# Where the weights of the quarter products begin in SBUF, and a shift of all SBUF operands by 32 bytes

## The chip, the core and the metric

The kernel runs on one core of one Trainium2 chip. The metric is the device time of one launch in microseconds. Inputs are already in the chip's memory (HBM), and the output goes back there. A core has TensorE (PE in the profile; its weight loads are listed apart as PEld), VectorE (DVE), ScalarE (ACT), GpSimd (POOL) and SyncE (SP), which here only issues DMAs. All of them work on SBUF, an on-chip memory of 128 partitions; an address below is a byte's place within a partition. Matmul results go to PSUM.

## The reference

A decoder trunk of two layers on 512 tokens of width 1024. Layer 0 mixes tokens with a gated delta rule, layer 1 with sliding-window attention; each layer then has a SwiGLU feed-forward block with an inner width of 2816. Cut to what matters here:

```
D_MODEL = 1024
SEQ = 512
D_FF = 2816
...
def swiglu(h, w_gate_up, w_down):
    gu = h @ w_gate_up
    return (jax.nn.silu(gu[..., :D_FF]) * gu[..., D_FF:]) @ w_down
...
    for layer in range(DEPTH):
        h = rms_norm(x, ln_mix[layer])
        ...
        x = x + jnp.concatenate([mix_out.astype(x.dtype), mem_o.astype(x.dtype)], axis=-1) @ w_out[layer]
        x = x + swiglu(rms_norm(x, ln_ffn[layer]), w_gate_up[layer], w_down[layer])
```

## The kernel before

Activations lie with features on partitions and tokens along the row: a tile of 128 features by 512 tokens. There are eight such tiles for the width of 1024. A product of such tiles runs on TensorE as a series of matmuls, each with a block of weights of 128 x 128 (the stationary operand, loaded into the array first) and a moving operand of up to 512 tokens.

To keep float32 accuracy, every large operand is split in two parts in a shorter float32 format (`fp32r`): a high part that ScalarE copies, and a low part that VectorE gets by subtraction (`split`, L168). `mm3` (L198) then multiplies with three matmuls: high weights with high activations, high weights with low, low weights with high. In the profile `g<-h,whi` is a matmul into PSUM tile g with moving operand h and weights whi; `l` and `wlo` are the low parts.

Three kinds of such matmuls fill the kernel:

- Full-width products, 512 tokens to a matmul: the projections of both layers, the output projection (`row`, `output`), part of the gate and up products and the whole down product (`ffn`, L1190 to L1198). The weights lie in tiles `whi` and `wlo` from `part` (L195), at the tile's beginning.
- Quarter products, 256 tokens to a matmul (`quarters`, L1275). Most of the gate and up products are made from seven products of half-size blocks in place of eight, with sums of weights and sums of activations. The moving operands are halves of h and of tiles T (the sums of activations, `token_sums`, L1246). One call makes two feature tiles with 7 x 4 x 3 = 84 matmuls; the two layers have 38 calls.
- Half-width products at the start (memory tokens) and at the very end (L1213 to L1222, the last two feature tiles of the down product, one half of the tokens at a time).

The weights of a quarter product are 512 elements wide, and two of them share a tile of 1152 elements (D + P). `ring` (L1130) hands out six such places. A place is a view of T + P = 640 elements, and the weights take 512 of them, beginning at element `shift[0]`:

```
places.extend(tuple(x[:, i * T:(i + 1) * T + P] for x in two) for i in range(2))
places.append(places.pop(0))
return [x[:, shift[0]:shift[0] + T] for x in places[-1]]
```

`begin` (L1139) sets `shift[0]` to P - 8 = 120 elements, 480 bytes, before the first weights are placed, so all of them begin there.

Tiles come from pools that are stacked from the left end of SBUF (constants, weights, activations, x) and from the right end (`side="right"`: what one stage alone needs, such as T). `build` (L246) opens the pools. The order of instructions on each engine is the order of the code, with a few orders added by hand (`nosync`, L116); a recording layer adds the waits that the tiles' overlaps require. SP's queue issues nearly all loads in order.

Every engine's order is settled when the program is built, and so is every address. In the built program before the change, moving operands of all full-width and quarter products begin at byte 320 modulo 512; weights of full-width products at 320; weights of quarter products at 288.

Of the kernel before, what the change touches and what calls it, by code (L numbers as in the profile page):

```python
# [9 lines left out]
F32 = mybir.dt.float32  # L10
# [8 lines left out]
P = 128  # L19
# [67 lines left out]
class Builder:  # L87
# [158 lines left out]
    def build(self):  # L246
        tc, nc, a = self.tc, self.nc, self.a
        with ExitStack() as st:
            opened = lambda name, **kw: tc.tile_pool(name=name, bufs=1, reuse_waits="tile", **kw)
            pool = lambda name, **kw: st.enter_context(opened(name, **kw))  # L250
            cp = pool("const")
            self.wpool, self.apool = pool("w"), pool("acta")
            self.dpool = pool("scratch", space=DRAM)
            self.load_constants(cp)
            self.weng = nc.vector
            with opened("layer0", side="right") as self.mpool:
                with self.banks(pj=3, g=2, sc=3):
                    with opened("early", side="right") as ep:
                        self.mem_and_norm(ep)
                    with opened("gdn", side="right") as gp:  # L260
                        mix = self.gdn(gp)
                    self.bpool, xp = pool("actb"), pool("x")
                    self.x = [self.t(xp, [P, T], F32, f"x{k}") for k in range(KD)]
                    for k in range(KD):
                        nc.sync.dma_start(self.x[k], a["xT"][:, k, :])
                    self.rstd, self.cosT, self.sinT = (self.t(xp, [P, T], F32, n) for n in ("rstd", "cosT", "sinT"))
                    h = self.output(xp, 0, mix)
            with opened("ffn0", side="right") as fp, self.banks(pj=2, g=6):
                self.ffn(fp, xp, 0, h, self.apool, rope=True)
            with self.banks(pj=2, qk=2, pt=2), opened("swa", side="right") as sp:  # L270
                h = self.output(xp, 1, *self.swa(sp))
            with opened("ffn1", side="right") as fp, self.banks(pj=2, g=6):
                self.ffn(fp, xp, 1, h, self.bpool)
# [825 lines left out]
    def ffn(self, fp, xp, layer, h, apool, rope=False):  # L1099
# [4 lines left out]
        acts, sums, open_pairs, places, waiting, shift, sized = [], [], [], [], [], [0], []  # L1104
# [34 lines left out]
        def begin(f, up, by, tag, bufs, then):  # L1139

            o = [self.t(fp, [P, T], F32, tag, bufs) for _ in range(2)]
            steps = self.quarters(fp, [col(f + i, up) for i in range(2)], sums, by, o, ring)
            shift[0] = P - 8
            next(steps)
            while waiting:
                x = waiting.pop()
                self.nosync(self.fn(x, x, AF.Silu), self.held)
            end()
            next(steps)
            open_pairs.append((steps, then, o))  # L1150
            return o

        def end():
            if open_pairs:
                steps, then, o = open_pairs.pop()
                next(steps, None)
                for x in o:
                    then(x)
# [8 lines left out]
        for f0 in (0, half):  # L1167
# [7 lines left out]
            for f in range(f0 + 1, f0 + half, 2):  # L1175
                if f == 1:
                    g = []
                    for i in range(2):
                        for _ in range(2 - i):
                            sums.append(self.token_sums(fp, layer, len(sums), h))  # L1180
                        g.append(gate(f + i))
                    sums.append(self.token_sums(fp, layer, len(sums), h))
                else:
                    g = begin(f, 0, (self.rstd, self.rstd), "fg", 4, lambda x: self.fn(x, x, AF.Silu))
                begin(f, 1, g, "fu", 3, put)
# [432 lines left out]
```

## Time and profile before

| | |
|---|---|
| Time, median of 3 runs | 1130.85 us (1130.81 to 1131.25) |
| Span of the profiled execution, first to last instruction | 1129.4 us |
| TensorE busy | 1119.9 us, 99%, 7339 matmuls |
| VectorE busy | 827.6 us, 73% |
| ScalarE busy | 634.4 us, 56% |
| DMA traffic | 151.15 MB, mean 134 GB/s |

The profile is of one execution, which has a span of its own; what lies around the span (the difference to the times of the runs) isn't in the trace. Durations of matmuls in the rows (279 ns with 256 columns, some 390 with 512) include the time in which a result runs through the array, and they overlap: the rate is read from the starts of neighbouring matmuls, or from a piece of the chain, which gives a length and a number of matmuls. In rows of groups, `x636 | 251.7, 398 | 0.0` means 636 instructions, 251.7 us busy together, 398 ns each, and no idle time of the engine ahead of them.

### The profile page before, as it was taken

To read this page: it belongs to the slowest core of one execution; us is meant where nothing else is said; L and a number is where in the kernel's file an instruction comes from. 1 tells how busy PE (TensorE), PEld (TensorE's weight loads), DVE (VectorE), ACT (ScalarE), POOL (GpSimd) and SP (SyncE) were. 2 spreads that over 40 slices of the span, in tenths; PEclk is the share of its full clock that TensorE was granted. 3 is DMA by queue.
4 is the path that set the end of the run, shared out by engine and by line. 5 is a ranking of instruction groups with operands and counts; after the bars stand their busy time and mean duration, and the time that the engine had idled before them with its cause. 6 is when DMAs were issued, how large, how long until landed. Compare 5 with 4: busy or idle time off the path is not lost.

```text
span 1129.4 us, 19330 instructions
## 1 busy us (share of the span) xinstructions
PE 1119.9 (99%) x7339; PEld 986.1 (87%) x7339; DVE 827.6 (73%) x1553; ACT 634.4 (56%) x1285; POOL 73.2 (6%) x91
## 2 busy tenths in 40 slices
PE   9999999999999999999999999999999999999997
PEld 8888778887899988899988887788999988999986
DVE  7676976577888975588955877839999634889643
ACT  8588664456566632366643555856666422666434
POOL 0000000000021001011000000000111000111001
PEclk9999999999999999999999999999999999999999
DMA  8344252234567536377533321116687533776232
GB/s 314 109 153 149 95 131 86 85 113 145 174 167 195 143 111 169 102 191 195 134 89 102 132 75 38 53 43 180 158 201 185 144 103 105 173 190 156 77 103 87
DMA packets 72401, 151.15 MB, mean 134 GB/s; under 512 B 16956, under 2 KB 18516, under 8 KB 72308
## 3 DMA queue, kind: packets, MB, share of 16 engines
q1 hardware_dynamic: 60884, 129.21, 36.3%
q0 software_dynamic: 11136, 20.45, 11.2%
q8 instruction: 57, 0.93, 0.3%
q14 instruction: 36, 0.29, 0.1%
q10 hardware_dynamic: 288, 0.26, 0.1%
HBM read 142.94 MB, written 6.96 MB: 133 GB/s over the span
## 4 chain that ended last, share of the span: by engine, by line
PE 96%; DVE 2%; ACT 1%; DMA 0%; issue 0%; DVEq 0%; SPq 0%; ACTq 0%
PE pj L146 46%; PE g L146 38%; PE sc L146 6%; PE qk L146 3%; PE pt L146 2%; PE pt L150 1%; PE g L150 1%; DVE big L153 1%; DVE qv L156 0%; DVE btmp L153 0%; DMA early<-in_early 0%; DVE wlo L153 0%; ACT sm L134 0%; DVE T L153 0%; DVE gcr L153 0%
## 5 line engine op out<-in xcount | busy, mean ns | idle before, releaser
L140 ACT ACTIVATE whi<-wraw 128x512 fp32r<-128x512 f32 (+3 forms) x318 | 235.3, 748 | 240.6 <-PE pj L146 164.0
L153 DVE TENSOR_TENSOR wlo<-wraw,whi 128x512 fp32r<-128x512 f32 (+3 forms) x318 | 262.8, 837 | 92.7 <-ACT whi L140 85.2
L146 PE MATMUL pj<-h,whi 128*128 128x512 f32 (+1 forms) x652 | 256.4, 395 | 0.0
L146 PE MATMUL pj<-l,whi 128*128 128x512 f32 (+1 forms) x652 | 254.4, 390 | 0.0
L146 PE MATMUL pj<-h,wlo 128*128 128x512 f32 (+1 forms) x652 | 254.0, 390 | 0.0
L146 PE MATMUL g<-T,whi 128*128 128x256 f32 x1216 | 216.8, 279 | 0.0
L146 PEld LDWEIGHTS g<-T,whi 128*128 128x128 f32 x1216 | 185.1, 188 | 1.3 <-DVE fu L156 1.3
L146 PE MATMUL g<-T,wlo 128*128 128x256 f32 x608 | 169.7, 279 | 0.0
L146 PEld LDWEIGHTS pj<-h,whi 128*128 128x128 f32 x652 | 122.4, 188 | 28.0 <-issue 4.1
L146 PEld LDWEIGHTS pj<-h,wlo 128*128 128x128 f32 x652 | 122.5, 188 | 25.4 <-issue 0.9
L146 PE MATMUL g<-l,whi 128*128 128x256 f32 (+1 forms) x500 | 144.5, 289 | 0.0
L146 PE MATMUL g<-h,whi 128*128 128x256 f32 (+1 forms) x500 | 144.4, 289 | 0.0
L146 PE MATMUL g<-h,wlo 128*128 128x256 f32 (+1 forms) x500 | 144.4, 289 | 0.0
L146 PEld LDWEIGHTS pj<-l,whi 128*128 128x128 f32 x652 | 122.6, 188 | 23.6 <-DVE l L1468 0.3
L146 PEld LDWEIGHTS g<-T,wlo 128*128 128x128 f32 x608 | 114.3, 188 | 0.0
L146 PEld LDWEIGHTS g<-h,whi 128*128 128x128 f32 x500 | 94.0, 188 | 1.9
L146 PEld LDWEIGHTS g<-l,whi 128*128 128x128 f32 x500 | 93.9, 188 | 1.9
L146 PEld LDWEIGHTS g<-h,wlo 128*128 128x128 f32 x500 | 93.9, 188 | 1.8
L1286 POOL DMA_DIRECT2D ws<-in_wgu x38 | 33.5, 881 | 733.0 <-DMA ws<-in_wgu 399.1
L140 ACT ACTIVATE whi<-ws 128x512 fp32r<-128x512 f32 x76 | 48.0, 631 | 42.0 <-PE g L146 35.6
L153 DVE TENSOR_TENSOR wlo<-ws,whi 128x512 fp32r<-128x512 f32 x76 | 52.0, 684 | 5.9 <-ACT whi L140 5.9
L1287 POOL DMA_DIRECT2D ws<-in_wgu x38 | 34.2, 900 | 196.4 <-DVE wlo L153 71.4
(421 smaller groups left out, 1683.2 us busy)
## 6 DMA issues: line engine op xcount, KB each, us to landing
wraw<-in_wgu SPq DMA_DIRECT2D x50, 512.0 KB, 4.4
ws<-in_wgu SPq DMA_DIRECT2D x76, 256.0 KB, 3.4
ws<-in_wgu POOLq DMA_DIRECT2D x76, 256.0 KB, 4.5
wraw<-in_win SPq DMA_DIRECT2D x26, 512.0 KB, 3.6
wraw<-in_wdn SPq DMA_DIRECT2D x32, 384.0 KB, 3.1
wraw<-in_wdn SPq DMA_DIRECT2D x32, 320.0 KB, 2.9
wraw<-in_wgu SPq DMA_DIRECT2D x38, 256.0 KB, 4.0
wraw<-in_wout SPq DMA_DIRECT2D x16, 512.0 KB, 3.6
```

Source lines behind the costliest of these rows:

```text
L140: self.copied = self.nc.scalar.activation(out, in_, AF.Copy, **kw).ins
L146: return self.nc.tensor.matmul(out, lhsT, rhs, start=start, stop=stop, skip_group_check=more).ins
L150: return self.nc.tensor.transpose(out, in_, self.ident[:k, :k]).ins
L153: return eng.tensor_tensor(out=out, in0=a, in1=b, op=op).ins
L1286: nc.gpsimd.dma_start(s1, a22, accum_op=ALU.add)
L1287: nc.gpsimd.dma_start(s3, a21, accum_op=ALU.add)
```

## The change

Two unused tiles are added. One of 8 elements (32 bytes) follows the opening of the pool of constants at the left end, so that all tiles behind it on that side begin 32 bytes further up. One of 120 elements (480 bytes) lies at the right end, so that all tiles on that side begin 480 bytes further down. Both are +32 modulo 512. `shift[0]` goes from 120 elements to 16: the quarter products' weights begin 64 bytes into their places, not 480.

```
@@ -248,7 +248,9 @@
             opened = lambda name, **kw: tc.tile_pool(name=name, bufs=1, reuse_waits="tile", **kw)
             pool = lambda name, **kw: st.enter_context(opened(name, **kw))
+            self.t(pool("edge", side="right"), [P, 120], F32, "edge")
             cp = pool("const")
+            self.t(cp, [P, 8], F32, "edge")
             self.wpool, self.apool = pool("w"), pool("acta")
...
@@ -1140,7 +1142,7 @@
             steps = self.quarters(fp, [col(f + i, up) for i in range(2)], sums, by, o, ring)
-            shift[0] = P - 8
+            shift[0] = 16
             next(steps)
```

In the built program the starts become, modulo 512:

| matmuls | number | moving operand | weights |
|---|---|---|---|
| full width, 512 columns | 2526 | 320, then 352 | 320, then 352 |
| quarter products, 256 columns | 3192 | 320, then 352 | 288, then 416 |
| half width at the end and start | 132 | 320, then 352 | 320, then 352 |
| half width at the start | 96 | 192, then 224 | 320, then 352 |
| half width at the start | 72 | 320, then 352 | 192, then 224 |
| half width at the start | 24 | 96, then 128 | 192, then 224 |

The instructions and their order stay the same on all engines. One wait is added, since the tiles from the left and those from the right now meet at another place. On SP's queue ahead of layer 0's output projection, the loads of x (the residual stream) and of the output weights stood so:

```order
105 L265 DMA x_524_2732<-in_xT 128x512 [waits DMAHW7_49]
106 L265 DMA x_525_2733<-in_xT 128x512 [waits DMAHW0_49]
107 L265 DMA x_526_2734<-in_xT 128x512 [waits DMAHW1_49]
108 L179 DMA wraw_2944<-in_wout 128x1024 [waits DMAHW2_49,DVE_49]
109 L179 DMA wraw_2984<-in_wout 128x1024 [waits DMAHW3_49,DVE_49]
```

In the same place on SP's queue they now stand so:

```order
105 L267 DMA x_526_2737<-in_xT 128x512 [waits DMAHW7_49]
106 L267 DMA x_527_2738<-in_xT 128x512 [waits DMAHW0_49]
107 L267 DMA x_528_2739<-in_xT 128x512 [waits DMAHW1_49,PE_49]
108 L179 DMA wraw_2949<-in_wout 128x1024 [waits DMAHW2_49,DVE_49]
109 L179 DMA wraw_2989<-in_wout 128x1024 [waits DMAHW3_49,DVE_49]
```

The last load of x (x7) now also waits for a matmul that reads the tile whose place it takes over.

More of the change, by code (lines that the diff above doesn't have):

```diff
@@ L250, in build @@
             pool = lambda name, **kw: st.enter_context(opened(name, **kw))
+            self.t(pool("edge", side="right"), [P, 120], F32, "edge")
             cp = pool("const")
+            self.t(cp, [P, 8], F32, "edge")
             self.wpool, self.apool = pool("w"), pool("acta")
@@ L1142, in begin @@
             steps = self.quarters(fp, [col(f + i, up) for i in range(2)], sums, by, o, ring)
-            shift[0] = P - 8
+            shift[0] = 16
             next(steps)
```

## The prediction

> **What bounds the kernel now.** I read the page first: the share of each engine, the chain of work that ended last, then the groups of instructions.
>
> ```profile
> span 1129.4 us, 19330 instructions
> PE 1119.9 (99%) x7339; PEld 986.1 (87%) x7339; DVE 827.6 (73%) x1553; ACT 634.4 (56%) x1285; POOL 73.2 (6%) x91
> PE 96%; DVE 2%; ACT 1%; DMA 0%; issue 0%; DVEq 0%; SPq 0%; ACTq 0%
> ```
>
> TensorE is busy for 99% of the span, and 96% of the chain that set the end runs through it. A busy share alone says little, since matmuls overlap; the list of what PE waited for is the better witness. It is this, whole:
>
> ```profile
> PE g L146 <- DVE eps L294: 1.2, 1, 1.2
> PE g L146 <- DVE DT L153: 0.4, 1, 0.4
> PE pj L146 <- ACT mh L140: 0.2, 1, 0.2
> ```
>
> Under 2 us in all. So nothing feeds TensorE too late, and the only way to a shorter time is a smaller distance from one matmul's start to the next one's. That distance stands in the chain, given in pieces with their length and their number of matmuls:
>
> ```profile
> 274.49 16.32 PE pj L146 x72
> 318.53 86.80 PE g L146 x744
> 407.51 64.65 PE pj L146 x285
> 801.60 86.80 PE g L146 x744
> 890.59 64.61 PE pj L146 x285
> ```
>
> In the quarter products (tile g, 256 columns) 744 matmuls take 86.80 us, 116.67 ns each, and in the second layer the same to the last digit. In the full-width products (tile pj, 512 columns) 72 take 16.32 us, 226.67 ns each; 285 take 64.65 us, 226.8 ns. The difference, 110 ns, buys 256 more columns. So 512 columns cost some 220 ns and every matmul, wide or narrow, loses a further 7 ns. Two matmuls of one width should therefore cost the same wherever their operands lie. They don't. Three stretches with 256 columns and no waits:
>
> ```profile
> 17.29 3.60 PE sc L146 x30
> 28.97 0.28 PE L146 MATMUL pj<-whi,ml 128*128 128x256 f32 x1
> ...
> 32.17 0.28 PE L146 MATMUL pj<-wlo,mh 128*128 128x256 f32 x1
> 1119.50 0.28 PE L146 MATMUL pj<-ac8h,T 128*128 128x256 f32 x1
> ...
> 1120.46 0.28 PE L146 MATMUL pj<-ac10h,T 128*128 128x256 f32 x1
> ```
>
> The first gives 3.60/30 = 120.0 ns. In the second, between the two rows lie 27 steps (28 matmuls, those two included): 3.20/27 = 118.5 ns. In the third, eight steps take 0.96 us: 120.0 ns. What differs is only where in SBUF the operands begin. From the addresses in the built program, as bytes modulo 512 (moving operand, then weights): the quarter products (320, 288) 116.67 ns; the first stretch (192, 320) 120.0; the second (320, 192) 118.5; the third (320, 320) 120.0. With the moving operand at 320 all three values occur, and with the weights at 320 the moving operand at 192 or at 320 makes no difference. So in these rows the start of the weights decides: 288 gives 116.67, 192 gives 118.5, 320 gives 120.0. 288 is the only one of the three that is an odd multiple of 32. The full-width products all stand at (320, 320), the dear place.
>
> **The change, part by part.** In the built program no instruction is added, removed or reordered on any engine. Addresses move: tiles on the left of SBUF by 32 bytes up, those on the right by 480 down, both +32 modulo 512. The extra +32 takes the moving operands of all large products from 320 to 352, and the weights of the full-width ones from 320 to 352. The quarter products' weights get their own move, from 480 to 64 bytes behind their tile's start: 288 becomes 416.
>
> Full-width products. The built program has 2526 of them; most stand in these rows:
>
> ```profile
> L146 PE MATMUL pj<-h,whi 128*128 128x512 f32 x636 | 251.7, 398 | 0.0
> L146 PE MATMUL pj<-l,whi 128*128 128x512 f32 x636 | 249.9, 393 | 0.0
> L146 PE MATMUL pj<-h,wlo 128*128 128x512 f32 x636 | 249.3, 392 | 0.0
> ```
>
> Their weights leave an even multiple of 32 (320) for an odd one (352). No row has 512 columns with weights at an odd multiple in a steady run, so the size is bounded from the narrow rows: at best the step from 120.0 to 116.67 ns, 3.33 ns less each, 2526 x 3.33 = 8.4 us; at worst, if 352 is as bad compared with 320 as 320 is compared with 288, 8.4 us more. I take the gain, because the dearer value was seen at 320 alone and every other start of weights was cheaper.
>
> Narrow products outside the quarters. 132 at (320, 320) at the end of the program and 96 at (192, 320) at its start go to weights at 352: 228 x 3.33 = 0.8 us less by the same step. 96 with weights at 192 go to 224: 96 x 1.83 = 0.2 us less if that too comes down to 116.67.
>
> Quarter products. Their count follows from these groups: 1216 + 608 + 3 x 456 = 3192.
>
> ```profile
> L146 PE MATMUL g<-T,whi 128*128 128x256 f32 x1216 | 216.8, 279 | 0.0
> L146 PE MATMUL g<-T,wlo 128*128 128x256 f32 x608 | 169.7, 279 | 0.0
> L146 PE MATMUL g<-l,whi 128*128 128x256 f32 x456 | 127.3, 279 | 0.0
> L146 PE MATMUL g<-h,whi 128*128 128x256 f32 x456 | 127.3, 279 | 0.0
> L146 PE MATMUL g<-h,wlo 128*128 128x256 f32 x456 | 127.3, 279 | 0.0
> ```
>
> Weights at 416 are again at an odd multiple of 32, and at the same place as 288 modulo 128. I take no change, 116.67 ns. Bounds: 3192 x 3.33 = 10.6 us more if they fall back to 120.0, and as much less if moving operand and weights together find one more such step.
>
> Everything else. The small float32 matmuls and transposes move too; they work in chains beside full-width products, and I count them at nothing. If they change by 3.33 ns as well, some 1300 of them are worth 4 us at most, either way; I keep that inside the range. VectorE and ScalarE have 27% and 44% of the span to spare by the page's first line, and PE's three waits on them come to 1.8 us, so a few ns on their operations are covered; were the cover gone, those waits would grow first.
>
> One wait is new: the last of eight loads of x on SP's queue (x7) now also waits for TensorE, since its tile overlaps another one differently. Behind it on SP stand the loads of the output weights and of the first gate weights, which need VectorE anyway.
>
> ```profile
> 255.46 0.39 PE L146 MATMUL sc<-R,Tt 128*128 128x128 f32 x2
> L265 SPq DMA_DIRECT2D x<-in_xT x8: 333/430/431, 263.3 to 266.5; - x8
> ```
>
> The matmul it waits for is one of the pair that starts at 255.46 us; the last load is issued at 266.5, 11 us later. Cost: nothing, and TensorE would have to be 11 us late in that one stage before it costs anything.
>
> The sum: 8.4 + 0.8 + 0.2 = 9.4 us; of this 96%, the chain's share on TensorE, counts: 9.0 us. The profiled execution spans 1129.4 us from first to last instruction and the median of the three runs is 1130.85, so 1.45 us lie around the span; they stay. 1130.85 - 9.0 = 1121.8 us.
>
> **A rule against it.** The rows say that two matmuls of equal width differ by 3.33 ns with the start of their weights. The Trainium skill, "TensorE: Matmul & The Clock Gate", section "Step-by-step: what each phase is for", says that TensorE reads moving operand and weights through two independent ports, and that loading the next weights takes no read bandwidth from the running matmul; "SBUF — State Buffer", section "Who interferes with whom", adds that "PE and ACT never wait on anyone". By that rule no shift of addresses would matter and the change would be worth 0. This trace doesn't agree as it stands: 116.67 against 120.0 ns. The same TensorE page, section "Wait — 56ns, not 53.3ns?", gives N/2.4 + 2.5 ns for back-to-back matmuls, an estimate of 109.2 and 215.8 ns here; the rows have 116.67 and 226.67, so they lie 7.5 and 10.9 ns above it.
>
> **The rivals.**
>
> It is the distance between the two operands that counts, not the start of the weights. Against: (192, 320) and (320, 320) cost the same with distances of 128 and 0. For: the one cheap place, (320, 288), is also the only one with the weights just 32 bytes below the moving operand. Then the full-width products, distance 0 before and after, gain nothing, and the quarter products, now 64 bytes apart, lose their good place and go to something between 118.5 and 120.0 ns: 3192 x 1.83 = 5.8 to 3192 x 3.33 = 10.6 us more; the middle, 8.2, gives 1139.0 us. It decides as soon as the quarter steps grow by more than 9.0 / 3192 = 2.8 ns while the full-width steps gain what I forecast, or by 0.7 ns if they gain nothing.
>
> Both gain: with all starts at odd multiples of 32, the quarters come down once more by 3.33 ns, 10.6 us on top of 9.4, together 20.0 us and with the 96% 19.2: 1111.6 us. For it: 116.67 ns is still 7 ns above the price of the columns. Against: no row shows a matmul of 256 columns below 116.67.
>
> Nothing changes: the differences between the stretches come from their surroundings (the first 33 us move more data, the last 16 us are in a part with waits) and not from addresses. Against: the stretch at 28.97 us and the one at 1119.50 have no wait inside, and each repeats its value evenly. Time: 1130.9 us. The rule of the skill above would give the same.
>
> Mixed: full-width gains 9.0, quarters lose 10.6: 1132.4 us, 0.14% above now.
>
> **How the numbers follow.** 0.38 for the forecast, 0.18 for both gain, 0.12 for nothing, 0.06 for mixed, 0.26 for the distance rule. 0.2% of the time, 2.3 us, is about what a measurement of this kernel can tell from no change. Faster: 0.38 + 0.18 = 0.56. Same: 0.12 + 0.06 = 0.18. Slower: 0.26. The forecast's own range is 1117 to 1127: half to one and a half of its gain. The range from 1111 to 1138 takes in both-gain at its price, nothing, mixed, and the lower half of the distance rule, and leaves out its upper half and what lies under 1111, less than 0.2 together.
>
> **What the next profile would show.** If I am right, the chain's piece of 744 quarter matmuls stays at 86.8 us in both layers, the piece of 285 full-width ones falls from 64.65 to about 63.7, and that of 72 from 16.32 to 16.08; the last stretch goes from 120.0 to about 116.7 ns. If the distance counts, the 744 take 88.2 to 89.3 us and the 285 stay. If both gain, the 744 take 84.3. If nothing changes, all stay. I am also wrong if PE's list of waits grows, or if the x7 load is issued late and the chain near 268 us goes through SP's queue.

## The result, and the profile after

The changed kernel takes 1134.26 us (median of 7 runs, 1133.70 to 1134.84); the kernel before took 1130.91 in the runs beside it (7 runs, 1130.62 to 1131.27). The ratio is 1.0030, with a 95% interval from 1.0020 to 1.0041: slower by 0.3%, some 3.4 us, where 9.0 us less were forecast. One execution of the shift alone, among the experiments below, took 2869.98 us and stands outside its median and ratio.

The page of the changed kernel: span and engines. These lines answer to the first ones shown of before.

```profile
span 1132.5 us, 19331 instructions
PE 1122.8 (99%) x7339; PEld 989.4 (87%) x7339; DVE 828.8 (73%) x1553; ACT 635.2 (56%) x1285; POOL 73.1 (6%) x91
```

The same 7339 matmuls keep TensorE busy 2.9 us longer, and the span is 3.1 us longer. What PE waited for, in the changed kernel (total, times, longest, in us):

```profile
PE g L146 <- DVE eps L296: 1.2, 1, 1.2
PE g L146 <- DVE DT L153: 0.4, 1, 0.4
PE g L146 <- DVE sqa L153: 0.3, 1, 0.3
```

Still under 2 us, so no wait has taken the place of another. The chain that ended last, in the changed kernel: start, length, and number of matmuls of each piece.

```profile
274.04 16.32 PE pj L146 x72
318.07 87.63 PE g L146 x744
407.86 64.62 PE pj L146 x285
472.49 102.96 PE g L146 x852
802.77 87.63 PE g L146 x744
892.54 64.62 PE pj L146 x285
957.17 102.96 PE g L146 x852
```

The pieces of 852 stood so in the kernel before:

```profile
472.16 102.05 PE g L146 x852
955.21 102.05 PE g L146 x852
```

The pieces of 744 quarter matmuls went from 86.80 to 87.63 us, in both layers alike: from 116.67 to 117.78 ns each. The pieces of 852 (840 quarter matmuls and a few others) went from 102.05 to 102.96. That makes 2 x (0.83 + 0.91) = 3.5 us, all of the difference. The full-width pieces did not move: 16.32 before and after, 64.62 against 64.65. Nor did the last stretch of half-width matmuls:

```profile
1122.61 0.28 PE L146 MATMUL pj<-ac8h,T 128*128 128x256 f32 x1
...
1123.57 0.28 PE L146 MATMUL pj<-ac10h,T 128*128 128x256 f32 x1
```

Eight steps in 0.96 us, 120.0 ns, the same as at the old addresses. The first stretch, 30 matmuls on tile sc, is again 3.60 us long. So wherever both operands moved by the same 32 bytes nothing changed, and only the quarter products changed, whose weights moved against their moving operands: from 32 bytes below them to 64 bytes above, modulo 512.

### The profile page after: what moved, and what is told of

Same layout as the page of the kernel before. It is cut to its first block, busy times and chain, and to the rows that moved or that the text cites. A ratio compares the mean times of both kernels' runs of the same rounds, so it can differ in the third digit from the quotient of the medians.

```text
span 1132.5 us, 19331 instructions
## 1 busy us (share of the span) xinstructions
PE 1122.8 (99%) x7339; PEld 989.4 (87%) x7339; DVE 828.8 (73%) x1553; ACT 635.2 (56%) x1285; POOL 73.1 (6%) x91
## 4 chain that ended last, share of the span: by engine, by line
PE 94%; DVE 3%; ACT 1%; DMA 1%; issue 0%; SPq 0%; DVEq 0%; ACTq 0%
PE pj L146 44%; PE g L146 38%; PE sc L146 6%; PE qk L146 3%; PE pt L146 2%; PE pt L150 1%; DVE big L153 1%; PE g L150 1%; DVE btmp L153 1%; DVE wlo L153 1%; ACT T L140 0%; DVE qv L156 0%; DMA early<-in_early 0%; DMA big<-basein 0%; ACT sm L134 0%
## 5 line engine op out<-in xcount | busy, mean ns | idle before, releaser
L146 PEld LDWEIGHTS g<-T,whi 128*128 128x128 f32 x1216 | 187.6, 190 | 1.2 <-DVE fu L156 1.2
```

Of the source, the lines that this page charges most:

```text
L146: return self.nc.tensor.matmul(out, lhsT, rhs, start=start, stop=stop, skip_group_check=more).ins
```

## The experiments

All kernels start from the kernel before, but for the first below and the changed kernel with four extra matmuls, which start from the changed one; none leaves work out. In the code, `...` marks lines left out. Rates that come from no quoted row are the mean distance between starts of neighbouring matmuls in the trace, over stretches of at least 11 without a wait. "Distance" is where the weights begin less where the moving operand begins, modulo 512 bytes; so 480 is -32.

**The unused tiles alone.** The two edge tiles of the change, with `shift[0] = P - 8` left as it was.

> The two unused tiles alone; the quarter products' weights stay 480 bytes into their places, so moving operands begin at 352 and weights at 320, and the distance from moving operand to weights is -32 as before. Theory D (the distance alone decides): 116.67 ns per quarter matmul, the piece of 744 at 86.80 us, time within 0.5 us of before, 1130.9. Rival S (the place where the weights begin decides, as the forecast had it): weights at 320 were dear before, so the quarters go to 120.0 ns, 3192 x 3.33 = 10.6 us more, 1141.5. Rival M (moving operands at 352 are what cost): 117.78 as in the changed kernel, 3.5 us more.

Measured: 1130.94 us, ratio 0.9999 (0.9989 to 1.0008). Its chain:

```profile
318.23 86.80 PE g L146 x744
407.22 64.65 PE pj L146 x285
801.35 86.80 PE g L146 x744
```

The weights of the quarters now begin at 320, the place that the forecast took to be dear, and the moving operands at 352; the rate is 116.67 ns as before. So neither of these two places counts by itself.

**The shift alone.** No unused tiles.

```
-            shift[0] = P - 8
+            shift[0] = 16
```

> The quarter products' weights 64 bytes into their places, no unused tiles: moving operands at 320, weights at 384, distance +64 as in the changed kernel. Theory D: 117.78 ns per quarter matmul, the piece of 744 at 87.63 us, 3192 x 1.11 = 3.5 us more than before, the same time as the changed kernel, 1134.3. Rival S: weights at 384, an even multiple of 32 and of 128; like 192 (118.5 ns) or 320 (120.0): 5.8 to 10.6 us more. Rival M: no change against before.

Measured: 1134.34 us (median of five), ratio 1.0030 (1.0017 to 1.0042), the changed kernel's time. Its chain:

```profile
318.77 87.63 PE g L146 x744
803.44 87.63 PE g L146 x744
```

The whole cost of the change is the new distance of +64. The 32-byte shift of both operands is worth nothing, either way.

**All distances in one run.** Each of the 38 calls of quarter products takes its own shift.

```
...
-            steps = self.quarters(fp, [col(f + i, up) for i in range(2)], sums, by, o, ring)
-            shift[0] = P - 8
+            s, self.calls = self.calls * 8 % (P + 8), self.calls + 1
+            steps = self.quarters(fp, [col(f + i, up) for i in range(2)], sums, by, o, lambda: ring(s))
```

> Each of the 38 calls of quarter products begins its weights at another place: 0, 32, 64, ... 512 bytes, going round, so every distance from 0 to 480 bytes is held by at least 168 matmuls in one run. Theory D: one value per distance, with 120.0 ns at 0, 116.67 at -32, 117.78 at +64, 118.5 at -128 and +96, 120.0 at +128, and the same value each time a distance comes back. Rival S: values by the start of the weights within 64 or 128 bytes, so a repeating pattern of two or four values. If the least is under 116.67, a better place exists; the whole is then bounded by 109, the 220/2 ns that 256 more columns cost in the profile of before.

Measured: 1144.13 us in one run. The rates, in ns, of steady stretches at each distance; where two stand, each held for whole stretches:

```
  0  119.9            128  118.5            256  119.9            384  118.5, 120.0
 32  118.3            160  120.0            288  118.3            416  119.8
 64  113.4, 117.8     192  113.4, 117.8     320  113.4, 117.8     448  117.8
 96  117.4, 120.0     224  116.7, 117.8     352  117.4, 120.0     480  117.8
```

Three things stand out. The least, 113.4 ns, lies well under the 116.67 of before. One distance can have two rates: +64 ran at 117.75 in one call and at 113.36 in another; and within single calls at 64, 192 and 320 it ran at 117.8 ahead of a stretch with some matmuls of the neighbouring call's distance and a few long steps (of 0.2 to 0.4 us), and at 113.3 behind it. And 480, that is -32, which gave 116.67 in the kernel before, ran at 117.8 here. One stretch at distance 320, 24 steps from the first row to the last:

```profile
494.47 0.28 PE L146 MATMUL g<-h,whi 128*128 128x256 f32 x1
...
497.07 0.28 PE L146 MATMUL g<-h,wlo 128*128 128x256 f32 x1
497.19 0.39 PE L146 MATMUL g<-T,whi 128*128 128x256 f32 x2
```

2.72 / 24 = 113.3 ns. The scan's own time is long because most distances are dear and the mixing adds short gaps.

**The same scan for full-width products.** Their weights begin 0, 32, ... 512 bytes into tiles that had the room.

```
...
-        hi, lo = (self.part(tag, bufs, pool)[:, :n] for tag in tags)
+        s = 0
+        if pool is None:
+            s, self.calls = self.calls * 8 % (P + 8), self.calls + 1
+        hi, lo = (self.part(tag, bufs, pool)[:, s:s + n] for tag in tags)
```

> Weights of full-width products begin 0, 32, 64, ... 512 bytes into their tiles, going round from one load to the next; quarters as before. Theory D: the same curve as for the quarters, so -32 saves 3.33 ns of the 226.67 and +64 saves 2.2. Rival W (512 columns hide the meeting of the two streams in another way): 226.67 everywhere, or another curve, with some distances over 226.67. Time within 10 us of before either way.

Measured: 1139.76 us in one run. The rival holds: another curve. Distance 0 mostly keeps 226.67 ns, 256 gives 226.7 to 230, 192 and 448 give some 229.5, and all others 232 to 234. The piece of 285 in this kernel, over a mixture of distances:

```profile
409.21 66.09 PE pj L146 x285
```

So full-width products already stood at their best distance, 0; at -32, the quarter products' good one, they would have cost some 7 ns more each (233.4 against 226.67).

**Distance 320 throughout.** `shift[0] = 80`, no unused tiles. The scan's rates at one distance now had two possible readings: a mean, or two states.

> Quarter products' weights 320 bytes into their places, no unused tiles, distance +320 throughout. In the scan this distance ran at 113.4 to 113.6 ns in three stretches and at 117.75 in one. Theory L (distance and how the run is entered decide together: at one distance the stream settles into one of two steady rates and keeps it): 113.4 ns in those blocks that settle low, 3192 x 3.3 = 10.5 us less, 1120.5, if all do; 3.5 us more, 1134.5, if none does; in between by blocks of 744 and 852 matmuls. Rival D1 (one value per distance, the scan's mean of 114.35): 3192 x 2.32 = 7.4 us less, 1123.5, with 114.35 everywhere.

Measured: 1134.16 us, ratio 1.0028 (1.0018 to 1.0038).

```profile
318.08 87.63 PE g L146 x744
472.50 102.96 PE g L146 x852
802.74 87.63 PE g L146 x744
957.16 102.96 PE g L146 x852
```

117.78 ns in all four blocks, not one stretch at 113.4, at the distance that gave 113.3 in the row above. The mean is refuted, and at this distance the low rate isn't had by the choice of distance alone. From here on, a distance's lower rate is called its low state and the upper one its high state.

**One extra small matmul per call.** Distance +64; ahead of each call's first matmul one of 8, 16, ... 128 columns, whose result the next one overwrites.

```
...
+            if extra:
+                self.mm(ps[:, :extra], w[0][:, :P], sums[0][b][0][:, :extra], True, True, True)
...
-        product(pa, a1[:, :T], "11", True)
+        self.calls += 1
+        product(pa, a1[:, :T], "11", True, 8 * (self.calls % 17))
```

> Distance +64 as in the changed kernel (weights 64 bytes into their places, no unused tiles), and ahead of each call's first matmul one extra matmul of 8, 16, 24, ... 128 columns (none in each 17th call), whose result the next one overwrites. Theory L: the extra matmul shifts the weight loads against the moving stream, so after some of them the rate is 113.36 ns and stays there until another shifts it back; both 113.36 and 117.78 are seen at this one distance. Rival D1: 117.78 everywhere but for the few matmuls around the extra one; time 1134.5 plus 36 x some 60 ns = 2 us.

Measured: 1132.91 us in one run, less than the changed kernel in spite of 36 more matmuls. Two neighbouring calls, behind the extra matmul of 8 columns and behind that of 16, at the same place of their products:

```profile
322.52 0.28 PE L146 MATMUL g<-h,whi 128*128 128x256 f32 x1
...
324.56 0.28 PE L146 MATMUL g<-h,whi 128*128 128x256 f32 x1
...
332.37 0.28 PE L146 MATMUL g<-h,whi 128*128 128x256 f32 x1
...
334.49 0.28 PE L146 MATMUL g<-h,whi 128*128 128x256 f32 x1
```

Between the rows of each pair lie 18 steps: 2.04 us, 113.3 ns, and 2.12 us, 117.8 ns. Within a call the rate did not change; it changed only at an extra matmul. The call that follows the full-width products ran low in all four blocks, behind 8, 80, 24 and 96 columns. A call behind a low one ran high in all cases but one (112 columns behind 104); behind a high one it ran low about every second time. So the number of columns alone doesn't decide: with 32 columns, a call behind a high one ran high in the first block and low in the last. Nor does the state ahead of it alone; what does isn't shown.

**Four blocks, four distances.** `shift[0] = (48, 112, 56, 88)[2 * layer + (f >= half)]`, no extra matmuls.

> One distance for each of the four blocks of quarter products (two in each layer): +192, +448, +224, +352, entered from full-width products as in the kernel before. In the scan +192 gave 117.8 and 113.36, +448 117.8 alone, +224 117.8 and 116.67, +352 120.0 and 117.4. Theory L: each block holds one of its distance's two values from its first matmuls to its last. Rival D1: the means of the scan, 116.4, 117.8, 117.2 and 118.6, by mixing within a block.

Measured: 1134.15 us in one run.

```profile
318.43 87.62 PE g L146 x744
472.90 102.96 PE g L146 x852
803.18 87.69 PE g L146 x744
957.68 102.60 PE g L146 x852
```

+192 held 117.78 and +448 held 117.78 from end to end, +352 held 117.33, the lower of its two. +224 began at 116.6 for 24 steps and, behind one step of 0.20 us, ran at 117.78 for 718: a state can be lost. Entered from full-width products without an extra matmul, none of these blocks reaches 113.4.

**The extra matmul once per block.** Distance +64, 24 columns, in the first call of each block only (`0 if open_pairs else 24` in place of the count).

> Distance +64 as in the changed kernel and one extra matmul of 24 columns ahead of the first quarter product of each of the four blocks, none elsewhere. In the kick scan the first kick of each block, entered from full-width products, was followed by 113.34 ns in all four blocks. Theory L: all 3192 run at 113.34 ns, the piece of 744 falls from 87.63 to some 84.3 us, and the time is 3192 x (116.67 - 113.34) = 10.6 us under before: 1120.3, and 14 us under the changed kernel. Rival K (the low rate needs kicks again and again and is lost within a block): between 1120.3 and 1134.5, with both rates inside a block. Rival D1: 1134.5.

Measured: 1124.66 us, ratio 0.9943 (0.9930 to 0.9957): 6.4 us less than before, not 10.6. The chain shows why:

```profile
317.68 84.45 PE g L146 x745
468.94 96.79 PE g L146 x830
795.85 20.53 PE g L146 x181
816.46 66.67 PE g L146 x564
949.91 93.98 PE g L146 x805
```

745 in 84.45 us is 113.35 ns; the third block starts the same way, 181 in 20.53 us, and then runs at 117.78. Between the two pieces the weight load of the 181st matmul comes late. The list names no releaser for it, only "issue"; but the row of VectorE shows what it waited for:

```profile
815.90 0.41 DVE L156 SCALAR_TENSOR_TENSOR fg<-g,fs 128x256 f32<-128x256 f32 x1
816.43 0.30 PEld L146 LDWEIGHTS g<-T,whi 128*128 128x128 f32 x2 [0.25 <-issue]
```

The 181st matmul is the first to add again to a sum in PSUM (`pa` in `quarters`) that this VectorE instruction reads, and in the built program it waits for this very instruction, which ends at 816.31 us. In the kernel before, the same instruction ended 0.44 us ahead of the matmul, in the changed kernel 0.58: a faster TensorE runs into VectorE here. Three blocks bear theory L out, and the third block is the mixed case of rival K, by one gap.

**The full-width scan with extra matmuls.** As the scan above, with 24 columns at the head of each full-width accumulation.

> The scan over distances of the full-width products again, with one extra matmul of 24 columns at the head of each such product's accumulation. Theory L: as with the quarters, some distances settle into another rate than the one seen without the extra matmul; if one lies under 226.67 ns, the full-width products too have a better place. Rival F (226.67 ns is the least that 512 columns take, whatever the entry): no distance under 226.67. Time some 1140 to 1150 either way, since most distances are dearer than 0.

Measured: 1150.87 us in one run. No distance went under the 226.67 ns that distance 0 had without extra matmuls: 228.4 at 0 (each product starts anew), 229.0 at 192, 229.2 at 256 and 448, some 233 to 234 elsewhere. Rival F stands for these entries.

**Extra matmuls at distance -32.** The scan over 8 to 128 columns with `shift[0] = P - 8`.

> Distance -32 as in the kernel before, with the extra matmul of 8, 16, ... 128 columns ahead of each call (none in each 17th). Theory L: calls run at 116.67 or at 117.78 ns, the two values that the scan and the kernel before showed at this distance, changing only at an extra matmul; none at 113.36. Rival D1: 116.67 throughout, time 1133.

Measured: 1136.33 us in one run. Calls ran at 116.7 or at 117.76 ns, and none at 113.4, as theory L had it. The 116.67 of the kernel before was the lower of two states at its distance.

**The changed kernel with four extra matmuls.** The change as it is, and 8 columns at the head of each block.

> The changed kernel as it is, with one extra matmul of 8 columns at the head of each of the four blocks. Theory L: all four blocks enter at 113.34 ns; in those that no gap in TensorE's stream disturbs, the rate holds: 1120.3 us if none is disturbed, some 1124.7 if one is disturbed as in the third block of the run with 24 columns. Rival A (the low rate belongs to the addresses without the unused tiles): 1134.3.

Measured: 1122.23 us, ratio 0.9926 (0.9911 to 0.9940).

```profile
318.19 84.44 PE g L146 x745
796.29 20.52 PE g L146 x181
816.85 64.18 PE g L146 x564
947.87 93.97 PE g L146 x805
```

The third block breaks at the same matmul, the 181st, behind the same VectorE instruction (which ends at 816.70 us), with a gap of 0.20 us in place of 0.25:

```profile
816.82 0.30 PEld L146 LDWEIGHTS g<-T,whi 128*128 128x128 f32 x2 [0.20 <-issue]
```

This time the stream fell back into the low state: 564 in 64.18 us, against 66.67 with 24 columns. Outside this gap the quarter products ran at 113.34 to 113.36 ns in all four blocks. This profile is of the fastest of four executions, 1121.71 us. One of the others took 1124.09: it was 2.4 us longer, about what the third block's rest costs in the high state (564 x 4.44 ns = 2.5 us). No trace shows that execution, so whether this block always falls back is open.

**80 columns, without the unused tiles.**

> No unused tiles, distance +64, one extra matmul of 80 columns at the head of each of the four blocks. Theory L: entry at 113.34 ns in all four blocks, as with 24 columns; 1120.4 us if no gap comes, some 1124.7 if the gap of 354 ns in the third block comes again at the same place of the program. If the gap is tied to the place in the program and not to the timing, it stands in the third call of the third block here too.

Measured: 1121.56 us, ratio 0.9918 (0.9902 to 0.9935).

```profile
318.05 84.46 PE g L146 x745
469.32 96.80 PE g L146 x830
796.20 84.69 PE g L146 x745
947.69 93.99 PE g L146 x805
```

Low in all four blocks. The 181st matmul of the third block again starts late, right behind VectorE (which ends at 816.63 us, the load starting at 816.68); the two steps there are 0.22 us longer together than two low ones, and the state holds. This and the one ahead are the fastest versions, 9.5 and 8.9 us below the kernel before; their intervals overlap. The forecast of 10.6 us less left out the price of the extra matmuls, some 0.11 us for each block from the last full-width matmul to the second quarter one.

## Why the prediction was wrong

- What bounds the kernel: right. TensorE's steps set the time before and after, and nothing else moved it.
- The step that failed: "So in these rows the start of the weights decides". It was read from four rates, each at a distance of its own (-32, 0, 128, -128), so that the distance fits them as well as the start of the weights does. The unused tiles alone refute it: weights at 320 ran at 116.67 ns when the moving operand stood at 352. Distance and state decide. What the step led to in the sum is the two terms that follow: a gain put on the full-width products, and nothing put on the quarter products.
- Full-width products, 8.4 us less: nothing came, 64.62 us against 64.65. Their distance stayed 0, and the scan shows that 0 is their best place. Assuming that a wide matmul follows the narrow one's rule was a second error: at -32 they would have gone up to 233.4 ns.
- Other half-width products, 1.0 us less: nothing, since their distances stayed; the last stretch took 120.0 ns before and after.
- Quarter products, no change: 1.11 ns more each, 3192 x 1.11 = 3.5 us more. This is the term that makes the whole result. 117.78 ns is the high state, which the run with extra matmuls at -32 shows there too; the change went from -32 in its low state to +64 in its high one.
- The x7 load's new wait, nothing: right. The load was issued at 266.1 us as the last of the eight, and PE's list of waits hardly grew (1.9 us against 1.8).

```profile
L267 SPq DMA_DIRECT2D x<-in_xT x8: 333/430/432, 262.9 to 266.1; - x8
```

- The rivals. That the distance counts was the right one, at 0.26. It was priced too high, at 8.2 us, since 118.5 to 120.0 ns were taken from other distances; +64 had 117.78. "Both gain" named 113.3 ns as a rate that the quarters might reach, on the ground that 116.67 was still above the price of the columns. The rate exists at this very distance, but that is luck: the ground was another one, and the changed kernel enters its blocks in the other state.
- The range held the time by luck: 1134.26 lies between the mixed case's 1132.4 and the distance rival's cheapest, 1130.85 + 5.8 = 1136.7, where no case had put it. The sign and the likeliest case were wrong.

The rule set against the change was that TensorE reads moving operand and weights through independent ports (the Trainium skill, "TensorE: Matmul & The Clock Gate", "Step-by-step: what each phase is for"). For a common shift of both operands its consequence holds, 0 us. For their distance it doesn't: 116.67 ns at -32 and 117.78 at +64 with nothing else changed, and 113.3 to 120.0 over all distances and states. The same page of the Trainium skill, "Wait — 56ns, not 53.3ns?", gives N/2.4 + 2.5 ns, an estimate of 109.2 ns for 256 columns; the least that any stretch here showed is 113.3.

What is shown: the rate depends on the distance between the operands and on a state that is set at entry, kept over hundreds of matmuls, and changed by a small matmul or by a gap. That the state is the timing of weight loads against the moving stream, and that reads of both meet in SBUF, was only argued; the starts in the trace don't tell the states apart, since a weight load is listed some 2 to 5 ns behind the start of a matmul in both. The gap at the 181st matmul of the third block is a wait for VectorE. What selects the low state behind a gap or an extra matmul stays open.

## What to carry to other kernels

In a stream of matmuls that never waits, read the step from start to start, and compare it among stretches of one width: in this kernel a few per cent hung on where weights begin against the moving operand, and a shift of both by 32 bytes was worth nothing here. Before choosing such a place by a single rate, look whether it holds throughout a long block and whether it returns after a disturbance: one distance had two steady rates here, 113.4 and 117.8 ns, and a matmul of 8, 24 or 80 columns at a block's head, some 0.11 us, chose the lower. A faster TensorE can then run into a wait that had been covered, as it did with VectorE in the third block. A rule found for one width is to be tried anew for another.

## What was not expected of the hardware

The two states are the surprise: 742 matmuls at 113.34 ns with an extra matmul ahead of them, and 743 at 117.78 without, at the same distance. The best distance of 256-column matmuls (64, 192 or 320 in the low state) is a poor one with 512 columns (about 233.5, 229.5 and 233.5 ns against 226.67 at 0). And within the quarter products the rates repeat at distances that differ by 256 almost throughout: 119.9 at 0 and 256, 118.3 at 32 and 288.
